# A two-layer model on one core: the second layer's mixer in three groups instead of two, in units tied to the expert stream

## The chip, the cores and the metric

The kernel runs on one core of a Trainium2 chip: TensorE (PE, with its weight loads as PEld), VectorE (DVE), ScalarE (ACT), GpSimd (POOL), SyncE (SP), and 16 DMA engines that all transfers share. The metric is the device time of one execution in microseconds.

## The reference

1024 tokens of width 1024 pass two layers and a last norm. Each layer is a mixer, then a feed-forward over experts ("PEER"). The first mixer is a gated linear recurrence (HGRN2), the second a stick-breaking attention over keys and values that are computed once from the first layer's output. Cut to what matters:

```python
for l in range(2):
    hn = modulate(rms_norm(h, norm_mix_g[l]), sh1, sc1)
    mix = hgrn2_mixer(hn, ...) if l == 0 else stick_breaking_mixer(hn, k_sh, v_sh, sb_w_q, sb_w_out)
    h = h + g1 * mix
    hn = modulate(rms_norm(h, norm_ffn_g[l]), sh2, sc2)
    h = h + g2 * peer_ffn(hn, peer_w_q[l], peer_subkeys[l], peer_u[l], peer_v[l])
    if l == 0:
        k_sh, v_sh = shared_kv(h, ...)       # 8 heads of 128
return rms_norm(h, final_norm_g)

def peer_ffn(xn, w_q, subkeys, u, v):        # per token: 4 heads x 16 experts of 16384
    sc = einsum(xn @ w_q, subkeys)           # 128 scores for each of 2 halves
    s1, i1 = top_k(sc[0], 16); s2, i2 = top_k(sc[1], 16)
    best, flat = top_k(s1[:, None] + s2[None, :], 16)
    w = softmax(best) * gelu(xn . u[expert])
    return sum(w * v[expert])

def stick_breaking_mixer(xn, k, v, w_q, w_out):   # block i of 128 queries sees key blocks 0..i
    z = q @ k.T;  a = exp(z + reversed cumulative sums of log_sigmoid(-z))
    return (a @ v) @ w_out
```

## The kernel before

The tokens are eight blocks of 128. Two things run side by side.

*The expert stream* (`peer_start`, `peer_rep`, `peer_quarter`) goes through the blocks of layer 0, then of layer 1, 16 blocks in all, each in four quarters of 32 tokens. A quarter gathers 16 times 128 table rows of 8 KB (u and v side by side), so 64 quarters make 1024 gathers of 1 MB. GpSimd issues a gather (L690) into a row tile `g`, VectorE multiplies the u half with the token's row `hq` and sums (L692), ScalarE makes Gelu and the scaled selection matrix `sel` for a pair of gathers (L694, L696), and TensorE adds the v half into `va` with four matmuls per gather, called sums here (L699). The tile is then free for a later gather. There are seven row tiles. Once a quarter ScalarE copies the rows of the next quarter's 32 tokens (L668).

*The rest* makes what the stream needs: the first mixer in groups of blocks (`G0`, `hgrn_group`, with routing in `mix_route`), and for the second layer `attn_group`. That one normalizes a group's blocks, projects queries (L730), then for each of eight heads projects keys (L747) and values (L751) of the group's blocks, stores them in DRAM for the later group (`kD`, `vD`), reads the older ones back, and runs `attn_head` for each block (L768 to L784). `mix_out` projects the output and adds it to `h`; `route_group` computes the routing scores (L552, L557) and `best_of` searches the 16 best on VectorE. Keys and values of a head, with two work areas, fill one head tile `K` of 16 KB per partition; there are two. Weights go through four `wt` tiles, 512 KB a load.

The order of instructions on each engine is made when the program is built: a list scheduler takes, among what it thinks ready, the instruction with the smallest priority, and `at(t)` sets the priority of what is written next. The stream's quarters carry the times of `pos`, 100 us ahead of a schedule of 207 us per block; a group's parts carry times spread evenly over its window in `W1`. `tc.issue_after(ins)` puts each instruction of the block behind `ins`, if it runs on the same engine as `ins`; it adds no wait.

Of the kernel before, what the change touches and what calls it, by code (L numbers as in the profile page):

```python
# [15 lines left out]
ALU = mybir.AluOpType  # L16
# [4 lines left out]
G0 = [[0, 1], [2, 3, 4], [5, 6, 7]]  # L21
G1 = [[0, 1, 2, 3], [4, 5, 6, 7]]
GH, GMAX = 3, 4
TAIL = 2
# [7 lines left out]
W0 = [(5, 230), (250, T0 + 2 * PERIOD - 25), (T0 + 1.8 * PERIOD, T0 + 5 * PERIOD - 60)]  # L32
W1 = [(T0 + 4.7 * PERIOD, T0 + 8.2 * PERIOD), (T0 + 7.9 * PERIOD, T0 + 11.8 * PERIOD)]


@with_exitstack
def tile_model(ctx, tc, x, cin, small, ada, w_in, w_out, kvada, kvw, sbq, sbo, wq, subk, tab0, tab1, out):
# [8 lines left out]

    BUFS = dict(wt=4, h=8, T=2, K=2, g=7, hn2=1, hq=2, gs=1, st=1)
    PBUFS = dict(ps=2, pj=2, po=1, pq=1, va=2)
# [38 lines left out]
    last = {}  # L87
# [198 lines left out]

    def mix_out(oT, blocks, w_ap, l, t0, t1):
        n = len(blocks)
        at(t0)
        for half in range(2):  # L290
            at(t0 + (t1 - t0) * half / 2)
            gsb = mix_row(l, half)
            ws = [wload(w_ap[4 * half + c]) for c in range(4)]
            for i, b in enumerate(blocks):
                at(t0 + (t1 - t0) * (half * n + i) / (2 * n))
                ps = bank()
                for c in range(4):
                    for k in range(8):
                        T.matmul(ps[:, blk(c)], lhsT=oT[:, k, blk(i)], rhs=ws[c][:, k, :], start=(k == 0), stop=(k == 7))  # L299
                V.tensor_tensor(out=ps, in0=gsb, in1=ps, op=ALU.mult)  # L300
                hh = hts[b][:, 512 * half:512 * half + 512]
                V.tensor_tensor(out=hh, in0=hh, in1=ps, op=ALU.add)

# [34 lines left out]
    def mix_route(oT, blocks, gsb, spare, t0, t1):  # L338
# [6 lines left out]
        held = spare + spare2 + parts(ktile())  # L345
        early_ws = []
        if blocks == G0[0]:
            work = [hts[7 - i] for i in range(n)]
            early_ws = hts[2:6]
        else:  # L350
            p = parts(ktile())
            work = p[:n]
            held += hts[blocks[-1] + 1:] + p[n:]
            early_ws = held[8:]
# [11 lines left out]

        early = 1 if len(held) >= 8 else n
        for half in range(2):
# [41 lines left out]
    def best_of(l, b, sc):  # L410
        eg = sm("eg", [128, 2, 64], bufs=GMAX)
        for j in range(8):
            if j % 2 == 0:
                s, ix = sm("s", [128, 2, 16]), sm("ix", [128, 2, 16], U32)
            top16(s[:, j % 2, :], ix[:, j % 2, :], sc[:, j], sc[:, j])
            if j % 2:
                pick(eg, j // 2, s, ix)
        R[l, b] = route(l, b, eg)
# [118 lines left out]

    def route_group(l, blocks, t0, t1):
        at(t0)
        n = len(blocks)  # L540
# [6 lines left out]
        for j in range(8):  # L547
            at(t0 + 0.4 * (t1 - t0) * j / 8)
            w = wload(wq[l, j])
            ps = bank("pj")  # L550
            for k in range(8):
                T.matmul(ps[:, 0:128 * n], lhsT=w[:, k, :], rhs=hT[:, k, 0:128 * n], start=(k == 0), stop=(k == 7))  # L552
            qr = sm("qr", [128, 128 * GMAX], bufs=1)
            S.copy(qr[:, 0:128 * n], ps[:, 0:128 * n])
            ps = bank()
            for i in range(n):
                T.matmul(ps[:, blk(i)], lhsT=qr[:, blk(i)], rhs=skt[:, j, :], start=True, stop=True)  # L557
            for i in range(n):
                S.copy(sc[i][:, j], ps[:, blk(i)])
        for i, b in enumerate(blocks):  # L560
            at(t0 + (t1 - t0) * (0.1 + 0.9 * i / n))
            best_of(l, b, sc[i])
# [110 lines left out]
    def peer_quarter(l, b, q):  # L673
# [6 lines left out]
        for c in range(0, 16, NC):  # L680
# [16 lines left out]
            for k in range(NC):  # L697
                for m in range(4):
                    T.matmul(va[32 * m:32 * m + 32, 0:256], lhsT=sel[:, k, :], rhs=ts[k][:, 1024 + 256 * m:1280 + 256 * m], start=(c + k == 0), stop=(c + k == 15))  # L699
        V.tensor_tensor(out=va[:, 0:256], in0=gates[l], in1=va[:, 0:256], op=ALU.mult)  # L700
# [11 lines left out]

    def attn_group(blocks, t0, t1):
        at(t0)
        d = t1 - t0
        n = len(blocks)
# [8 lines left out]
        for j in range(8):  # L725
            at(t0 + d * (0.02 + 0.09 * j / 8))
            w = wload(sbq[j])
# [5 lines left out]
        for i in range(n):  # L733
            norm_T(hs[i], hT[:, :, blk(n - 1 - i)], modk[:, 8:16], modk[:, 0:8], rev=True)
        for hd in range(8):
            at(t0 + d * (0.12 + 0.58 * hd / 8))
            kt = ktile()
# [17 lines left out]
            for i, b in enumerate(blocks):  # L755
                attn_head(b, qT[:, hd, blk(i)], kh, vh, th, st)
        mix_out(qT, blocks, sbo, 1, t0 + 0.7 * d, t0 + 0.8 * d)
        route_group(1, blocks, t0 + 0.8 * d, t1)

# [57 lines left out]

    order = [(l, b) for l in range(2) for b in range(8)]
    with tc.issue_after(norm00[0]):
        peer_start(*order[0])  # L820
    peer_rep(*order[0], 0)
    for n, (l, b) in enumerate(order):
        for q in range(4):
# [5 lines left out]
            peer_quarter(l, b, q)  # L829
        for grp, w in zip(G1, W1):  # L830
            if l == 0 and grp[-1] == b:
                attn_group(grp, *w)

# [63 lines left out]
```

## Time and profile before

| | |
|---|---|
| median of three runs | 3625.27 us (3622.58 to 3629.86) |
| profiled execution, its time | 3632.76 us |
| its span | 3631.1 us |
| PE busy | 2585.4 us, 71% |
| DVE busy | 2600.6 us, 72% |
| ACT, POOL busy | 1127.5 us, 1523.5 us |
| moved by DMA | 1272.86 MB, of it 1073.81 MB by gathers |
| mean granted TensorE clock | 0.805 |

No engine is busy for more than three quarters of the span, but the share of each changes from one stretch to the next, so a share over the whole span names no limit.

### The profile page before, as it was taken

To read this page: it belongs to the slowest core of one execution; us is meant where nothing else is said; L and a number is where in the kernel's file an instruction comes from. 1 tells how busy PE (TensorE), PEld (TensorE's weight loads), DVE (VectorE), ACT (ScalarE), POOL (GpSimd) and SP (SyncE) were. 2 spreads that over 40 slices of the span, in tenths; PEclk is the share of its full clock that TensorE was granted. 3 is DMA by queue.
4 is the path that set the end of the run, shared out by engine and by line. 5 is a ranking of instruction groups with operands and counts; after the bars stand their busy time and mean duration, and the time that the engine had idled before them with its cause. 6 is when DMAs were issued, how large, how long until landed. Compare 5 with 4: busy or idle time off the path is not lost.

```text
span 3631.1 us, 52700 instructions
## 1 busy us (share of the span) xinstructions
PE 2585.4 (71%) x18916; PEld 1654.3 (46%) x18916; DVE 2600.6 (72%) x6229; ACT 1127.5 (31%) x2959; POOL 1523.5 (42%) x1691
## 2 busy tenths in 40 slices
PE   5787999878998888988933488788797333343433
PEld 4686666665767745557411135455573111111111
DVE  7949777599776896665799546766757985565555
ACT  2114332233322443333333233333333232222221
POOL 3322656335664333224334433343343444444443
PEclk8898999899999999999955589899998555555555
DMA  9845989897999899888889988887898899999998
GB/s 394 347 143 221 354 344 359 336 352 303 358 361 365 337 344 372 326 337 328 342 349 353 414 352 351 346 328 309 320 381 345 333 373 409 419 415 418 416 416 349
DMA packets 203878, 1272.86 MB, mean 351 GB/s; under 512 B 22626, under 2 KB 22754, under 8 KB 72547
## 3 DMA queue, kind: packets, MB, share of 16 engines
q0 software_dynamic: 147456, 1073.81, 74.6%
q1 hardware_dynamic: 56162, 195.69, 14.3%
q8 instruction: 152, 2.49, 0.3%
q14 instruction: 108, 0.88, 0.1%
HBM read 1261.02 MB, written 8.39 MB: 350 GB/s over the span
## 4 chain that ended last, share of the span: by engine, by line
PE 42%; DVE 28%; issue 13%; POOL 6%; DMA 6%; ACT 5%; POOLq 0%; SPq 0%; DVEq 0%; ACTq 0%; another core or an unknown queue 0%
DVE g L692 8%; PE pj L445 7%; PE va L699 6%; POOL g L690 5%; DMA g<-in_tab_dram,ev 5%; PE pj L730 3%; PE ps L299 3%; PE pj L747 3%; PE pj L552 3%; PE ps L362 2%; ACT hq L668 2%; PE pj L751 2%; PE pj L449 2%; PE po L783 2%; DVE g L215 2%
## 5 line engine op out<-in xcount | busy, mean ns | idle before, releaser
L690 POOL DMA_INDIRECT g<-in_tab_dram,ev x1024 | 1200.7, 1173 | 1720.1 <-PE va L699 1129.0
L692 DVE SCALAR_TENSOR_TENSOR g<-g,hq 128x1024 f32<-128x1024 f32 x1024 | 1260.7, 1239 | 298.7 <-DMA g<-in_tab_dram,ev 287.5
L699 PE MATMUL va<-g,sel 128*32 128x256 f32 x8192 | 751.0, 499 | 772.4 <-ACT sel L696 764.3
L699 PEld LDWEIGHTS va<-g,sel 128*32 128x32 f32 x8192 | 256.7, 132 | 1191.5 <-ACT sel L696 989.3
L694 ACT ACTIVATE w<-hid 128x2 f32<-128x2 f32 x512 | 104.2, 204 | 1293.2 <-DVE g L692 1274.5
L445 PE MATMUL pj<-T,wt 128*128 128x384 f32 (+1 forms) x1152 | 358.7, 462 | 0.0
L668 ACT COPY hq<-hn 32x1024 f32<-32x1024 f32 x256 | 266.8, 1042 | 44.6 <-DVE g L692 40.4
L696 ACT ACTIVATE sel<-dg,w 128x32 f32<-128x32 f32 x1024 | 273.0, 314 | 15.6
L445 PEld LDWEIGHTS pj<-T,wt 128*128 128x128 f32 x1152 | 216.6, 195 | 101.3 <-issue 7.2
L685 DVE TENSOR_TENSOR dg<-delta,gt 128x128 f32<-128x128 f32 x256 | 78.1, 305 | 179.7 <-ACT sel L696 179.2
L494 POOL TENSOR_TENSOR K<-K,F 128x384 f32<-128x384 f32 (+1 forms) x144 | 151.4, 1071 | 52.9 <-DVE T L466 35.4
L215 DVE SCALAR_TENSOR_TENSOR g<-g,hn 128x1024 f32<-128x1024 f32 x104 | 129.2, 1266 | 6.1 <-DMA g<-in_ada_dram 6.1
L449 PE MATMUL pj<-wt,T 128*128 128x128 f32 x1024 | 127.5, 280 | 0.7 <-ACT K L451 0.6
L751 PE MATMUL pj<-wt,T 128*128 128x128 f32 x1024 | 126.3, 277 | 0.0
L751 PEld LDWEIGHTS pj<-wt,T 128*128 128x128 f32 x1024 | 120.0, 192 | 12.7 <-issue 10.6
L449 PEld LDWEIGHTS pj<-wt,T 128*128 128x128 f32 x1024 | 120.5, 194 | 8.8 <-issue 3.7
L299 PE MATMUL ps<-wt,T 128*128 128x128 f32 x1024 | 123.8, 280 | 0.0
L299 PEld LDWEIGHTS ps<-wt,T 128*128 128x128 f32 x1024 | 118.3, 194 | 11.3 <-issue 9.5
L747 PE MATMUL pj<-T,wt 128*128 128x512 f32 x256 | 120.3, 619 | 0.0
L730 PE MATMUL pj<-T,wt 128*128 128x512 f32 x256 | 117.3, 610 | 2.1 <-DVE T L277 2.1
L552 PE MATMUL pj<-T,wt 128*128 128x512 f32 x256 | 116.2, 604 | 0.5 <-DVE T L277 0.5
L783 PE MATMUL po<-K 128*128 128x128 f32 x576 | 104.5, 329 | 15.4 <-ACT K L781 14.9
(239 smaller groups left out, 3896.2 us busy)
## 6 DMA issues: line engine op xcount, KB each, us to landing
wt<-in_w_in_dram SPq DMA_DIRECT2D x96, 512.0 KB
g<-in_ada_dram SPq DMA_DIRECT2D x88, 512.0 KB
g<-in_tab_dram,ev POOLq DMA_INDIRECT x1024
wt<-in_kvw_dram SPq DMA_DIRECT2D x32, 512.0 KB
wt<-in_w_out_dram SPq DMA_DIRECT2D x18, 512.0 KB
wt<-in_wq_dram SPq DMA_DIRECT2D x17, 512.0 KB
g<-in_kvada_dram SPq DMA_DIRECT2D x16, 512.0 KB
wt<-in_sbq_dram SPq DMA_DIRECT2D x16, 512.0 KB
```

The costliest lines, as they stand in the source:

```text
L299: T.matmul(ps[:, blk(c)], lhsT=oT[:, k, blk(i)], rhs=ws[c][:, k, :], start=(k == 0), stop=(k == 7))
L445: T.matmul(pw, lhsT=w[:, k, :], rhs=hT[:, k, 0:W], start=(k == 0), stop=(k == 7))
L449: T.matmul(ps[:, blk(i)], lhsT=hT[:, k, blk(i)], rhs=w[:, k, :], start=(k == 0), stop=(k == 7))
L552: T.matmul(ps[:, 0:128 * n], lhsT=w[:, k, :], rhs=hT[:, k, 0:128 * n], start=(k == 0), stop=(k == 7))
L668: S.copy(t[32 * j:32 * j + 32, :], hn2[32 * q:32 * q + 32, :])
L690: G.indirect_dma_start(out=t, out_offset=None, in_=tab, in_offset=bass.IndirectOffsetOnAxis(ap=ev[:, q, c + k:c + k + 1], axis=0))
L692: V.scalar_tensor_tensor(u, u, 1.0, hq, op0=ALU.mult, op1=ALU.mult, accum_out=hid[:, k:k + 1])
L696: S.activation(sel[:, k, :], dg[:, c % 4 + k, :], AF.Copy, scale=wt[:, k:k + 1])
L699: T.matmul(va[32 * m:32 * m + 32, 0:256], lhsT=sel[:, k, :], rhs=ts[k][:, 1024 + 256 * m:1280 + 256 * m], start=(c + k == 0), stop=(c + k ...
L730: T.matmul(ps[:, 0:W], lhsT=w[:, k, :], rhs=hT[:, k, 0:W], start=(k == 0), stop=(k == 7))
L747: T.matmul(ps[:, 0:W], lhsT=w[:, k, :], rhs=hT[:, k, 0:W], start=(k == 0), stop=(k == 7))
L751: T.matmul(ps[:, blk(i)], lhsT=hT[:, k, blk(i)], rhs=w[:, k, :], start=(k == 0), stop=(k == 7))
```

## The change

- `G1` is three groups, blocks 0 to 2, 3 to 5, and 6 and 7, where there were two of four blocks. `GMAX` falls from 4 to 3, and with it the size of the tiles `T`, which hold a group's transposed rows.
- `K` has three tiles instead of two, the row tiles `g` are six instead of seven.
- `attn_group` is a generator of twelve units: norms and queries, eight heads, two halves of the output projection, routing. From quarter 17, 29 and 41 on (counted from 0), each group gives one unit per quarter, written behind the quarter's instructions with the priority of the quarter's end, and with its TensorE instructions behind the last sum of that quarter (`last["va"]`).
- In the first layer `mix_route` takes one more head tile for early loads of weights (not for the last group); the part `early` gets is 1, 1 and n as before.

The diff, cut to its core:

```diff
-G1 = [[0, 1, 2, 3], [4, 5, 6, 7]]
-GH, GMAX = 3, 4
+G1 = [[0, 1, 2], [3, 4, 5], [6, 7]]
+GH, GMAX = 3, 3
-W1 = [(T0 + 4.7 * PERIOD, T0 + 8.2 * PERIOD), (T0 + 7.9 * PERIOD, T0 + 11.8 * PERIOD)]
+S1 = [17, 29, 41]
-    BUFS = dict(wt=4, h=8, T=2, K=2, g=7, hn2=1, hq=2, gs=1, st=1)
+    BUFS = dict(wt=4, h=8, T=2, K=3, g=6, hn2=1, hq=2, gs=1, st=1)
...
+        if blocks != G0[2]:
+            held += parts(ktile())
...
-        early = 1 if len(held) >= 8 else n
+        early = 1 if len(held) > 8 else n
...
-                    T.matmul(va[32 * m:32 * m + 32, 0:256], lhsT=sel[:, k, :], rhs=ts[k][:, 1024 + 256 * m:1280 + 256 * m], start=(c + k == 0), stop=(c + k == 15))
+                    last["va"] = T.matmul(va[32 * m:32 * m + 32, 0:256], lhsT=sel[:, k, :], rhs=ts[k][:, 1024 + 256 * m:1280 + 256 * m], start=(c + k == 0), stop=(c + k == 15)).ins
...
+        yield
         for hd in range(8):
-            at(t0 + d * (0.12 + 0.58 * hd / 8))
...
                 attn_head(b, qT[:, hd, blk(i)], kh, vh, th, st)
-        mix_out(qT, blocks, sbo, 1, t0 + 0.7 * d, t0 + 0.8 * d)
-        route_group(1, blocks, t0 + 0.8 * d, t1)
+            yield
+        for half in range(2):
+            mix_half(qT, blocks, sbo, 1, half)
+            yield
+        route_group(1, blocks)
+        yield
...
+    work = [(first, attn_group(grp)) for first, grp in zip(S1, G1)]
...
-        for grp, w in zip(G1, W1):
-            if l == 0 and grp[-1] == b:
-                attn_group(grp, *w)
+            slot = 4 * n + q
+            for first, group in work:
+                if slot >= first:
+                    at(T0 + PERIOD * (slot + 1) / 4)
+                    with after("va"):
+                        next(group, None)
```

What this does to TensorE's order is seen at two places. The first is a head of the second group before: its key projection (`pj`, 512 columns) and value projection stand among the sums of the stream (`va`), whichever quarter these belong to.

```order
L780 MATMUL ps_16536<-ident,K_16411 128x128 x3
L783 MATMUL po_16529<-K_16411 128x128 x4
L747 MATMUL pj_16586<-T_15996,wt_16583 128x512 x8
L783 MATMUL po_16529<-K_16411 128x128 x2
L699 MATMUL va_19384<-g_19452,sel_19451 32x256 x4
L699 MATMUL va_19384<-g_19455,sel_19451 32x256 x4
L699 MATMUL va_19384<-g_19474,sel_19473 32x256 x4
L699 MATMUL va_19384<-g_19477,sel_19473 32x256 x4
L783 MATMUL po_16529<-K_16411 128x128
L751 MATMUL pj_16599<-wt_16596,T_15996 128x128 x14
```

In the change a head's unit of the first group (lines have moved: sums are L694, keys L740, values L744) begins right behind the last sum of one quarter (`va_11529`) and ahead of the first pair of the next (`va_11799`); three pairs of sums farther on its values are done, and the last pairs of the quarter have nothing ahead of them.

```order
L694 MATMUL va_11529<-g_11684,sel_11680 32x256 x4
L740 MATMUL pj_11706<-T_10878,wt_11704 128x384 x8
L744 MATMUL pj_11719<-wt_11717,T_10878 128x128 x2
L694 MATMUL va_11799<-g_11805,sel_11804 32x256 x4
L694 MATMUL va_11799<-g_11808,sel_11804 32x256 x4
L744 MATMUL pj_11719<-wt_11717,T_10878 128x128 x2
L694 MATMUL va_11799<-g_11825,sel_11824 32x256 x4
L694 MATMUL va_11799<-g_11828,sel_11824 32x256 x4
L744 MATMUL pj_11719<-wt_11717,T_10878 128x128 x20
L765 MATMUL pj_11746<-K_11703,T_10781 128x128
```

The second place is TensorE's order in quarter 47, the last of block 3 of layer 1. Before, the second layer's other work is behind it there, and only sums and a row for the stream's own input are left.

```order
L699 MATMUL va_21718<-g_21724,sel_21723 32x256 x4
L699 MATMUL va_21718<-g_21727,sel_21723 32x256 x4
L184 MATMUL pq_22256<-ident,modc_167 128x128 x4
L699 MATMUL va_21718<-g_21744,sel_21743 32x256 x4
L699 MATMUL va_21718<-g_21747,sel_21743 32x256 x4
L699 MATMUL va_21718<-g_21766,sel_21765 32x256 x4
```

In the change a head of the third group stands there, between the pairs of sums.

```order
L740 MATMUL pj_20848<-T_19454,wt_20845 128x256 x8
L744 MATMUL pj_20861<-wt_20858,T_19454 128x128
L694 MATMUL va_20999<-g_21005,sel_21004 32x256 x4
L694 MATMUL va_20999<-g_21008,sel_21004 32x256 x4
L744 MATMUL pj_20861<-wt_20858,T_19454 128x128 x5
L694 MATMUL va_20999<-g_21025,sel_21024 32x256 x4
L694 MATMUL va_20999<-g_21028,sel_21024 32x256 x4
L744 MATMUL pj_20861<-wt_20858,T_19454 128x128 x10
L765 MATMUL pj_20879<-K_20844,T_19357 128x512
L765 MATMUL pj_20882<-K_20844,T_19357 128x384
```

On SP's queue the second group of the change both reads stored keys and values and writes its own, so reads into a head tile, writes out of one and weight loads take turns. Before, the group that read wrote nothing.

```order
L736 DMA K_16533<-kD 128x384
L736 DMA K_16533<-vD 128x384
L94 DMA wt_16548<-in_kvw_dram 128x1024
L747 DMA vD<-K_15933 128x384
L736 DMA K_16908<-kD 128x384
L736 DMA K_16908<-vD 128x384
L94 DMA wt_16909<-in_kvw_dram 128x1024
L747 DMA kD<-K_16233 128x384
L94 DMA wt_16923<-in_kvw_dram 128x1024
```

A write stands ahead of loads for the heads that follow.

## Rows read from the trace of the kernel before

**Rows 1.** Stretches: PE, PEld, DVE, ACT, POOL busy us (records); clock; DMA share; GB/s.

```profile
300.00:1322.00 1022.00, 904.09 (x6817) 654.78 (x6817) 822.12 (x2148) 354.30 (x926) 506.67 (x653) 0.94 0.87 335
1322.00:1776.00 454.00, 404.55 (x2846) 262.14 (x2844) 291.55 (x686) 158.37 (x417) 155.37 (x144) 0.95 0.90 344
1776.00:1982.00 206.00, 96.64 (x699) 41.05 (x698) 198.43 (x695) 66.45 (x167) 80.95 (x69) 0.62 0.90 348
1982.00:2104.00 122.00, 48.86 (x432) 17.01 (x432) 70.23 (x129) 32.17 (x88) 57.98 (x52) 0.53 1.00 404
2104.00:2770.00 666.00, 571.39 (x3966) 366.60 (x3966) 433.73 (x798) 234.71 (x617) 252.69 (x212) 0.93 0.86 338
2770.00:2966.00 196.00, 76.01 (x624) 28.88 (x622) 185.97 (x647) 57.07 (x145) 83.38 (x70) 0.57 0.90 348
2966.00:3600.00 634.00, 251.74 (x2148) 83.12 (x2144) 367.43 (x662) 163.29 (x456) 292.88 (x269) 0.52 1.01 415
```

**Rows 2.** The same stretches, gather issues alone (L690): the count stands in brackets.

```profile
1322.00:1776.00 454.00, 143.93 (x128) 0.95 0.90 344
1776.00:1982.00 206.00, 78.33 (x65) 0.62 0.90 348
1982.00:2104.00 122.00, 57.02 (x50) 0.53 1.00 404
2104.00:2770.00 666.00, 239.25 (x190) 0.93 0.86 338
2770.00:2966.00 196.00, 80.86 (x65) 0.57 0.90 348
2966.00:3600.00 634.00, 285.57 (x251) 0.52 1.01 415
```

**Rows 3.** Timeline around a key projection: start, us, what, [idle before and releaser].

```profile
2354.69 7.98 PE L747 MATMUL pj<-T,wt 128*128 128x512 f32 x16
...
2363.99 0.94 POOL L690 DMA_INDIRECT g<-in_tab_dram,ev  x1 [13.26 <-PE va L699]
...
2370.83 1.22 DVE L692 SCALAR_TENSOR_TENSOR g<-g,hq 128x1024 f32<-128x1024 f32 x1
```

**Rows 4.** Waits: GpSimd's in 2104 to 2770, VectorE's for landings in 300 to 1322.

```profile
POOL g L690 <- PE va L699: 290.8, 64, 13.9
...
DVE g L692 <- DMA g<-in_tab_dram,ev: 7.8, 7, 2.8
```

**Rows 5.** Stretches, sums alone (L699): PE, PEld busy, clock, DMA share.

```profile
1322.00:1776.00 454.00, 73.03 (x1010) 27.42 (x1010) 0.95 0.90 344
2104.00:2770.00 666.00, 107.66 (x1520) 41.36 (x1520) 0.93 0.86 338
2966.00:3600.00 634.00, 239.00 (x2004) 73.88 (x2000) 0.52 1.01 415
```

**Rows 6.** DMA issues by SP: KB each.

```profile
wt<-in_kvw_dram SPq DMA_DIRECT2D x32, 512.0 KB
...
kD<-K SPq DMA_DIRECT2D x8, 256.0 KB
```

**Rows 7.** Groups by line, TensorE, 2104 to 2770 (four blocks): busy, mean ns, idle before.

```profile
L730 PE MATMUL pj<-T,wt 128*128 128x512 f32 x128 | 58.2, 606 | 0.0
...
L270 PE MATMUL ps<-ident,K 128*128 128x128 f32 x40 | 8.2, 362 | 6.9 <-ACT T L275 4.7 <-ACT K L256 1.7 <-DVE h L302 0.4
```

**Rows 8.** Timeline of the stream alone, with the row copies of a quarter.

```profile
3204.16 1.26 POOL L690 DMA_INDIRECT g<-in_tab_dram,ev  x1 [2.44 <-PE va L699]
...
3205.88 1.23 DVE L692 SCALAR_TENSOR_TENSOR g<-g,hq 128x1024 f32<-128x1024 f32 x1 [1.26 <-DMA g<-in_tab_dram,ev]
...
3209.14 1.27 POOL L690 DMA_INDIRECT g<-in_tab_dram,ev  x1 [2.47 <-PE va L699]
...
3212.37 4.20 ACT L668 COPY hq<-hn 32x1024 f32<-32x1024 f32 x4
...
3218.97 0.96 POOL L690 DMA_INDIRECT g<-in_tab_dram,ev  x1 [0.33 <-PE va L699]
```

More of the change, by code (lines that the diff above doesn't have):

```diff
@@ L285, in mix_row, with mix_half @@
         return g
[L287 to L302, printed above, removed]
+    def mix_half(oT, blocks, w_ap, l, half):
+        gsb = mix_row(l, half)
+        ws = [wload(w_ap[4 * half + c]) for c in range(4)]
+        for i, b in enumerate(blocks):
+            ps = bank()
+            for c in range(4):
+                for k in range(8):
+                    T.matmul(ps[:, blk(c)], lhsT=oT[:, k, blk(i)], rhs=ws[c][:, k, :], start=(k == 0), stop=(k == 7))
+            V.tensor_tensor(out=ps, in0=gsb, in1=ps, op=ALU.mult)
+            hh = hts[b][:, 512 * half:512 * half + 512]
+            V.tensor_tensor(out=hh, in0=hh, in1=ps, op=ALU.add)
     state = unit("st", (128, 8, 128))
@@ L410, in best_of @@
     def best_of(l, b, sc):
-        eg = sm("eg", [128, 2, 64], bufs=GMAX)
+        eg = sm("eg", [128, 2, 64], bufs=4)
         for j in range(8):
@@ L536, in tile_model, with route_group @@
     norm00, norm7, best0 = [], [], []
-    def route_group(l, blocks, t0, t1):
-        at(t0)
+    def route_group(l, blocks):
         n = len(blocks)
@@ L547, in route_group @@
         for j in range(8):
-            at(t0 + 0.4 * (t1 - t0) * j / 8)
             w = wload(wq[l, j])
@@ L560, in route_group @@
         for i, b in enumerate(blocks):
-            at(t0 + (t1 - t0) * (0.1 + 0.9 * i / n))
             best_of(l, b, sc[i])
@@ L711, in tile_model, with attn_group @@
     vD = dp.tile([8, 128, 8, 128], F32, name="vD")
-    def attn_group(blocks, t0, t1):
-        at(t0)
-        d = t1 - t0
+    def attn_group(blocks):
         n = len(blocks)
@@ L725, in attn_group @@
         for j in range(8):
-            at(t0 + d * (0.02 + 0.09 * j / 8))
             w = wload(sbq[j])
```

## Prediction

> **What bounds the kernel now.** Start with the table of stretches [rows 1] and read one column at a time. In the last stretch and in the short one at 1982 the DMA share is 1.00 to 1.01: nothing else matters there. The gathers issued in these two [rows 2], 50 and 251 in 122 and 634 us, give the price of one gather at full DMA rate, 756/301 = 2.51 us, so 40.2 us for a quarter of 16. Elsewhere the DMA share is 0.86 to 0.90, and each stretch has another limit. In 1322 to 1776 and 2104 to 2770 it is TensorE: busy 404.55 of 454 and 571.39 of 666 us, at a granted clock of 0.95 and 0.93, with VectorE at 64 and 65%. In 1776 to 1982 and 2770 to 2966 it is VectorE, 198.43 of 206 and 185.97 of 196 us: the top-16 searches of four blocks. The first layer, 300 to 1322, has TensorE at 88% and VectorE at 80%.
>
> What each stretch costs beyond 2.51 us per gather, from the counts in [rows 2]: the two TensorE stretches 454 - 128 x 2.51 = 132.7 and 666 - 190 x 2.51 = 189.1, together 321.8 us; the two VectorE stretches 206 - 65 x 2.51 and 196 - 65 x 2.51, together 75.7 us.
>
> How a TensorE stretch loses its time is seen in one place [rows 3]. At 2354.69 a head's key projection occupies TensorE for 7.98 us; the sums queued behind it come after it, and only at 2363.99 can GpSimd, idle for 13.26 us, reuse a row tile and issue a gather. The total of that wait in the second stretch is 290.8 us [rows 4].
>
> **The change, part by part.**
>
> *Spreading.* TensorE's second-layer work is what is not a sum in the two stretches: 404.55 - 73.03 and 571.39 - 107.66 [rows 1, 5], 795 us. It is not made smaller: three groups do the same blocks with the same columns. It now lies in 36 quarters (three times twelve units), 22 us each. A quarter's sums are 128 records (a matmul stands as two in this profile) of 107.66/1520 us at the high clock, 9.1 us. So 31 us of TensorE against 40.2 of gathers: TensorE is no longer the limit of a light quarter, and the 321.8 us fall away, if nothing else takes their place. What does is priced next.
>
> *Loads.* Three groups instead of two load every second-layer weight a third time: 16 for the key and value weights, 8 each for query, output and routing queries, 1 for subkeys, so 41 of 512 KB [rows 6] or 21.5 MB. The stored keys and values go from 32 transfers of 256 KB to 32 writes and 16 reads of 192 KB and 16 reads of 384 KB, 15.7 for 8.4 MB. The second layer's loads are then 123 x 0.524 + 15.7 = 80.2 MB. Behind a busy TensorE their time was covered; in quarters that DMA limits it is not: 80.2 MB at 415 GB/s [rows 1] is 193 us. The VectorE stretches left a tenth of 402 us of DMA free; half of that, 20 us, I let cover loads: +173. Ends: 69 us (only the 28.8 MB that are new count) and 193. On SP a write of stored keys waits for ScalarE's copy, and weight loads of the next heads stand behind it, as the order shows; four weight tiles and three head tiles keep these a head ahead, so I add nothing. A load that came late all the same would hold one key projection and the sums behind it.
>
> *First units.* Query projection and transposes of three blocks are one unit. From [rows 7] the projection is 58.2 x 3/4 = 43.7 us and 24 transposes and 24 reversals, priced alike at 8.2/40, are 9.8; with the sums 63 us, 16 above a light quarter of some 47. For the first group I count it whole, for the others half, as these quarters are VectorE's (the searches of the group before) anyway: +32. Ends 0 and 48.
>
> *Searches.* The same VectorE work in three bursts: 75.7 us as now.
>
> *Six row tiles.* In [rows 8] the cycle of a pair is seen at full DMA rate: a pair's first gather is issued at 3204.16, the next pair's at 3209.14, 5.0 us later. How short could a tile's cycle be? With an almost empty queue a gather issued at 2363.99 is multiplied at 2370.83 [rows 3], 6.84 us; its partner lands 2.51 later; and from the second multiply (3205.88) to the next issue (3209.14) [rows 8] are 3.26 us. Sum 12.6. Six tiles are three pairs, 15.06 us at full rate, so 2.5 us are to spare; seven tiles had 17.57, so 5.0. Once a quarter the four copies that spread the next quarter's rows stand on ScalarE ahead of the pair's weights: 4.20 us at 3212.37, and the next issue comes at 3218.97 instead of some 3214.1. Seven tiles cover 4.2 us, six leave 1.7 open. There are 46 quarters from 18 on (counted from 0); without 8 that VectorE limits: +66. Ends 0 (the spare is larger than I measured) and, if ScalarE's and VectorE's other waits also come through, the rival below.
>
> The Trainium skill has a fixed price for such a transfer: "DMA: Bandwidth & Descriptors", section on the anatomy of one DMA by the GpSimd path, gives about 2.0 us plus bytes over 436e3, estimated 4.4 us for a 1 MB gather. By it the cycle would be some 10.2 us, six tiles would cover the copies, and the forecast would be 66 us lower. The trace has 6.84 us up to the multiply, and its number is the one used.
>
> *Key projections behind the quarter's last sum.* In the change they stand where the order shows them, once a quarter, 7.98 x 3/4 = 6.0 us (4.0 in the group of two). The first pair of sums is due 5.0 us after the last one, so about 1 us is late: 24 x 1 = +24. Ends 0 and, if each still cost the 13.26 - 5.0 us of [rows 3], 198.
>
> *First layer.* Six row tiles and a third head tile. VectorE waited for a gather's landing only 7.8 us in those 1022 [rows 4]: gathers lie ready, so one tile less should cost nothing. TensorE's order holds the same work ahead of quarter 16; it is idle 118 us, of which a third head tile might return a third. I take 0, ends -40 and +50; the startup loads, which find two half row tiles fewer, and the routing weights, which find four more places, lie inside these ends.
>
> *Sum.* -322 + 173 + 32 + 66 + 24 = -27 us. The profiled execution took 3632.8 us, so 3606; it stands 7.5 us above the median of the three runs, which gives **3598 us**.
>
> **Rivals.**
>
> *All cheap (faster).* Six tiles and the projections cost nothing, and half of the first units: 3598 - 66 - 24 - 16 = 3492; half-way to that is 3545. For it: VectorE's few waits in the first layer. Against: at full rate it waits for each landing already [rows 8].
>
> *Nothing gained.* Loads, first units and tiles eat up what spreading frees: 27 us more of costs than I count, which is one more microsecond in each light quarter. 3625.
>
> *Six tiles make the second layer wait (slower).* In 2104 to 2770 one gather takes 666/190 = 3.5 us, so a tile's cycle was 7 x 3.5 = 24.5 us, twice the 12.6 it could be; the rest is waiting in the queues of TensorE, ScalarE and VectorE [rows 4]. A light quarter of 47.4 us needs a cycle of at most 6 x 47.4/16 = 17.8 us. That is where it decides: each microsecond above adds 16/6 = 2.7 us to a quarter, 80 us over some 30 light quarters. At 18.9, still nearer to 12.6 than to 24.5, the kernel takes 3598 + 85 = 3683.
>
> *The clock (slower).* In the stretches without second-layer work TensorE's granted clock is 0.52 to 0.62, the lower of its levels (1.2 of 2.4 GHz) nearly throughout, and a sum costs 239.00/2004 us instead of 107.66/1520 [rows 5], 1.68 times as much. If light quarters ran so, TensorE would need 31 x 1.68 = 52 us in each, 4.7 more than 47.4, and over 30 of them 140. Against it: a projection is a dense run, and in [rows 1] such work ran at 0.93 and 0.95. With half of it at the low level: 3598 + 70 = 3668.
>
> The Trainium skill, "TensorE: Matmul & The Clock Gate", section on HAM oscillation in real kernels, speaks against the change here: matmul chunks shorter than the DMA waits between them run at the throttled clock, chunk after chunk. By it the whole 140 us would come; the trace shows the low clock only where sums stand alone.
>
> **How the numbers follow.** The forecast and its neighbourhood, 3570 to 3617, gets 0.38; cheap, below 3570, 0.16; nothing gained, within 0.2% of 3625 (about what a measurement of this kernel can tell from no change), 0.11; six tiles 0.22; clock 0.13. So faster 0.54, same 0.11, slower 0.35. The range 3510 to 3700 leaves one in ten at each end: below lies most of "all cheap" together, above the full price of the clock or a cycle over 19 us. If it is faster, 3530 to 3617.
>
> **What the new profile would show.** Right: DMA share 0.95 or more in most of the second layer outside the searches, GpSimd's wait for sums without pieces of 13 us, quarters of some 47 us in the light ones, and the end of the run at full DMA rate with little above 41 us a quarter. Wrong: VectorE waiting for landings with a DMA share below 0.9 (six tiles); sums at over 0.11 us each and a clock near 0.5 in the light quarters (clock); a first layer that ends later than now, at which I look first; or searches that are not done when the second layer's stream reaches their blocks, which would stop the gathers outright.

## The result and the profile after

The changed kernel takes 3678.84 us (median of four runs, 3672.47 to 3684.18) beside 3627.57 us for the kernel before in the same comparison: a ratio of 1.0148, interval [1.0135, 1.0161]. It is slower, where 3598 was forecast. The time is near that of the rival in which six row tiles make the second layer wait, 3683, but it did not come about in that way, as the section on the prediction shows. The profiled execution took 3676.5 us, its span is 3674.7.

In the view of stretches the second layer of the changed kernel, from 1323 on, falls into light quarters (one unit of a group in each) and short bursts, in which searches and the first unit of the next group lie. The columns are those of [rows 1]: PE, PEld, DVE, ACT, POOL busy; clock; DMA share; GB/s.

```profile
300.00:1323.00 1023.00, 883.73 (x6694) 639.83 (x6694) 827.93 (x2194) 338.73 (x893) 505.89 (x647) 0.92 0.87 335
1323.00:1471.00 148.00, 106.83 (x716) 59.28 (x717) 85.23 (x174) 48.73 (x129) 58.04 (x50) 0.80 0.93 367
1471.00:1966.00 495.00, 332.27 (x2508) 205.75 (x2508) 286.10 (x593) 149.65 (x407) 193.48 (x177) 0.75 0.96 374
1966.00:2150.00 184.00, 151.59 (x937) 91.97 (x935) 164.96 (x551) 71.89 (x177) 53.98 (x50) 0.90 0.88 339
2150.00:2601.00 451.00, 328.53 (x2504) 216.42 (x2505) 287.50 (x541) 151.46 (x404) 184.54 (x164) 0.83 0.96 374
2601.00:2785.00 184.00, 132.35 (x895) 90.29 (x893) 166.22 (x541) 65.17 (x168) 64.85 (x53) 0.86 0.89 345
2785.00:3125.00 340.00, 215.94 (x1726) 145.98 (x1726) 214.73 (x362) 104.78 (x278) 141.41 (x119) 0.78 0.96 380
3125.00:3279.00 154.00, 93.86 (x740) 61.48 (x740) 118.69 (x362) 50.44 (x133) 61.44 (x57) 0.75 0.95 372
3279.00:3640.00 361.00, 135.34 (x1136) 43.78 (x1136) 210.53 (x413) 87.78 (x247) 163.06 (x144) 0.51 0.97 391
```

The same stretches behind the first layer with the gather issues alone (L685 here), the count in brackets, answer to [rows 2]:

```profile
1323.00:1471.00 148.00, 57.07 (x48) 0.80 0.93 367
1471.00:1966.00 495.00, 185.00 (x161) 0.75 0.96 374
1966.00:2150.00 184.00, 52.15 (x48) 0.90 0.88 339
2150.00:2601.00 451.00, 175.06 (x144) 0.83 0.96 374
2601.00:2785.00 184.00, 61.40 (x48) 0.86 0.89 345
2785.00:3125.00 340.00, 138.05 (x112) 0.78 0.96 380
3125.00:3279.00 154.00, 57.98 (x48) 0.75 0.95 372
3279.00:3640.00 361.00, 159.89 (x136) 0.51 0.97 391
```

Read the DMA share first. Before, the stretches with second-layer work showed 0.86 and 0.90 and TensorE was busy for 86 to 89% of them; now the light ones show 0.96 and TensorE is busy for 64 to 73%. The work has been spread as intended and no other engine is at its limit, yet the DMA engines are not full either. In the last stretch, where the stream runs alone, the share was 1.01 and is now 0.97: 361 us for 136 gathers is 42.5 us a quarter, where [rows 1, 2] give 634/251 x 16 = 40.4.

By the ledger of the prediction (time less 2.51 us per gather):

- the three light stretches, 1286 us and 417 gathers: 239 us, 49.3 us a quarter. At the 47.4 that I forecast they would have cost 188;
- the two bursts at 1966 and 2601: 127; the start at 1323 and the third burst at 3125: 27.5 and 33.5. Together 188, where the forecast left 168 (371 less the 188 above and 15 for the last stretch);
- the last stretch: 19.6, forecast 15.

So 51 + 20 + 5 = 76 us too much, of which some 5 came back elsewhere: the profiled time is 70 us above the 3606 that the sum gave for it. The first layer ends as before: the first 260 gathers are issued by 1268 us, before it was 261 by 1269.

What is missing in a light quarter is read from the waits in 1471 to 1966 (engine, line, waited for: us, times, longest).

```profile
POOL g L685 <- PE va L694: 204.6, 56, 8.9
...
DVE g L687 <- DMA g<-in_tab_dram,ev: 116.7, 83, 7.2
```

VectorE waits 116.7 us for landings while the DMA engines have a share of 0.96: gathers are issued too late, since GpSimd waits for row tiles. One quarter's start in the timeline shows how.

```profile
1763.25 0.95 POOL L685 DMA_INDIRECT g<-in_tab_dram,ev  x1 [0.30 <-issue]
...
1764.89 4.20 ACT L663 COPY hq<-hn 32x1024 f32<-32x1024 f32 x4
...
1769.12 0.53 ACT L691 ACTIVATE sel<-dg,w 128x32 f32<-128x32 f32 x2
...
1769.49 1.94 PE L694 MATMUL va<-g,sel 128*32 128x256 f32 x16 [7.34 <-ACT sel L691]
...
1771.36 6.76 PE L740 MATMUL pj<-T,wt 128*128 128x384 f32 x16
...
1771.39 0.53 ACT L691 ACTIVATE sel<-dg,w 128x32 f32<-128x32 f32 x2
...
1771.49 0.97 POOL L685 DMA_INDIRECT g<-in_tab_dram,ev  x1 [0.33 <-PE va L694]
...
1773.24 1.00 POOL L685 DMA_INDIRECT g<-in_tab_dram,ev  x1 [0.17 <-issue]
...
1778.49 1.07 PE L694 MATMUL va<-g,sel 128*32 128x256 f32 x16
...
1779.43 0.95 POOL L685 DMA_INDIRECT g<-in_tab_dram,ev  x1 [5.20 <-PE va L694]
```

ScalarE copies the next quarter's rows for 4.20 us; only then come the weights (1769.12), and TensorE has sat idle for 7.34 us when the last sums of the quarter start. Behind them the key projection takes 6.76 us (predicted 6.0). The weights of the next pair are ready at 1771.92, yet its sums start only at 1778.49, 6.6 us later. The issue at 1763.25 is the second of a pair, and the next pair's second comes at 1773.24, 10.0 us later; from this pair's first, at 1771.49, to the first of the following one are 7.9 us. 5.0 would keep the DMA engines busy [rows 8]. Here six tiles had no reserve for two such delays on end.

### The profile page after: what moved, and what is told of

Read it like the earlier page. It is cut to its first block, busy times and chain, and to the rows that moved or that the text cites. A ratio compares the mean times of both kernels' runs of the same rounds, so it can differ in the third digit from the quotient of the medians.

```text
span 3674.7 us, 53571 instructions
## 1 busy us (share of the span) xinstructions
PE 2620.5 (71%) x19308; PEld 1761.3 (48%) x19308; DVE 2603.9 (71%) x6229; ACT 1138.4 (31%) x2993; POOL 1533.6 (42%) x1691
## 3 DMA queue, kind: packets, MB, share of 16 engines
q1 hardware_dynamic: 66674, 224.53, 16.2%
q8 instruction: 155, 2.54, 0.3%
## 5 line engine op out<-in xcount | busy, mean ns | idle before, releaser
L685 POOL DMA_INDIRECT g<-in_tab_dram,ev x1024 | 1207.6, 1179 | 1723.9 <-PE va L694 1105.4
L694 PE MATMUL va<-g,sel 128*32 128x256 f32 x8192 | 725.8, 484 | 759.9 <-ACT sel L691 759.3
L694 PEld LDWEIGHTS va<-g,sel 128*32 128x32 f32 x8192 | 250.2, 128 | 1119.8 <-ACT sel L691 952.1
L443 PE MATMUL pj<-T,wt 128*128 128x384 f32 (+1 forms) x1152 | 357.2, 462 | 0.7 <-DVE T L278 0.7
L740 PE MATMUL pj<-T,wt 128*128 128x384 f32 (+1 forms) x384 | 143.7, 527 | 3.7 <-DVE T L278 2.7
L744 PEld LDWEIGHTS pj<-wt,T 128*128 128x128 f32 x1024 | 125.1, 192 | 22.5 <-issue 15.2
L744 PE MATMUL pj<-wt,T 128*128 128x128 f32 x1024 | 132.9, 279 | 0.0
L780 PE MATMUL po<-K 128*128 128x128 f32 x576 | 117.9, 371 | 20.9 <-ACT K L778 20.5
L780 PEld LDWEIGHTS po<-K 128*128 128x128 f32 x576 | 102.6, 269 | 43.0 <-ACT K L778 38.0
L548 PE MATMUL pj<-T,wt 128*128 128x384 f32 (+1 forms) x384 | 118.1, 457 | 6.1 <-DMA wt<-in_wq_dram 3.5
```

Of the source, the lines that this page charges most:

```text
L443: T.matmul(pw, lhsT=w[:, k, :], rhs=hT[:, k, 0:W], start=(k == 0), stop=(k == 7))
L685: G.indirect_dma_start(out=t, out_offset=None, in_=tab, in_offset=bass.IndirectOffsetOnAxis(ap=ev[:, q, c + k:c + k + 1], axis=0))
L694: last["va"] = T.matmul(va[32 * m:32 * m + 32, 0:256], lhsT=sel[:, k, :], rhs=ts[k][:, 1024 + 256 * m:1280 + 256 * m], start=(c + k == 0), ...
L740: T.matmul(ps[:, 0:W], lhsT=w[:, k, :], rhs=hT[:, k, 0:W], start=(k == 0), stop=(k == 7))
L744: T.matmul(ps[:, blk(i)], lhsT=hT[:, k, blk(i)], rhs=w[:, k, :], start=(k == 0), stop=(k == 7))
L780: T.matmul(po[:, 0:128], lhsT=vh[:, 7 - b + j, :], rhs=st[:, blk(j)], start=(j == 0), stop=(j == n - 1))
```

## The experiments

Ratios are to the kernel before on the same chip, in brackets the 95% interval. Runs on different chips are compared by their ratios, a ratio of 0.01 being 36 us. The kernel before itself took 3627.6 to 3644.5 us in these comparisons, so times read from the traces of two of them can differ by 0.5% without meaning anything. "The units" means groups, units and their place behind the sums, as in the change.

**Row tiles and head tiles.** Three kernels keep the units, go back to two head tiles and take six, seven and eight row tiles. Without the third head tile the early loads of the first layer's routing have no extra places, and `early` is n throughout. The first is shown; the others have `g=7` and `g=8`. Eight row tiles and two head tiles fill the same memory as the change's six and three.

```diff
-    BUFS = dict(wt=4, h=8, T=2, K=3, g=6, hn2=1, hq=2, gs=1, st=1)
+    BUFS = dict(wt=4, h=8, T=2, K=2, g=6, hn2=1, hq=2, gs=1, st=1)
...
-        if blocks != G0[2]:
-            held += parts(ktile())
...
-        early = 1 if len(held) > 8 else n
+        early = n
```

Six row tiles:

> The change with two head tiles instead of three and still six row tiles (the first layer's early weight loads go back to their old places, and all of a group's output halves are done before its routing). It is the control for the next two. Theory (six row tiles cost the second layer its gain): 3665 to 3700, like the change, since the row tiles are the same. Rival (the third head tile was what the change needed): above 3700, with the second layer's heads waiting for a tile.

Measured 3706.52 us, 1.0221 [1.0204, 1.0238], just above 3700 and so in the range of the rival. What was missing is shown further down: not the tile for the heads, but the places for early loads.

Seven:

> The same with seven row tiles, as many as before. Theory (six row tiles): 65 to 75 us less than with six: the ten quarters at the end go from 43 back to 41 us (20 us), some 29 light quarters from 49 to 47.5 (45 us); about 3610. Rival (row tiles do not matter; the loads of a third group and the quarters in which searches and first units meet do): within 15 us of the control.

Measured 3599.09 us, 0.9923 [0.9907, 0.994], a gain of 107 us where 65 to 75 were expected.

Eight:

> The same with eight row tiles, in the memory that the kernel before used. Theory (six row tiles): a little below the one with seven, 3590 to 3610, because four whole pairs are in flight; the DMA share of light quarters near 1.00. Rival: within 15 us of the control.

Measured 3576.40 us, 0.9856 [0.984, 0.9873], below the expected range.

One tile is worth 107 us from six to seven, 23 from seven to eight. The stretch of ten light quarters (20 to 29) is shown by the view of stretches, for each kernel the row of all engines, then that of its gather issues. Six tiles:

```profile
1485.00:1982.00 497.00, 333.71 (x2487) 208.14 (x2487) 281.70 (x581) 149.56 (x407) 190.28 (x175) 0.74 0.94 368
1485.00:1982.00 497.00, 180.96 (x159) 0.74 0.94 368
```

Seven:

```profile
1458.00:1926.00 468.00, 326.52 (x2503) 204.26 (x2504) 283.70 (x591) 149.35 (x407) 190.09 (x176) 0.77 0.99 395
1458.00:1926.00 468.00, 178.90 (x160) 0.77 0.99 395
```

Eight:

```profile
1473.00:1924.00 451.00, 324.68 (x2509) 205.35 (x2510) 281.95 (x591) 149.78 (x408) 192.77 (x176) 0.79 1.00 406
1473.00:1924.00 451.00, 181.62 (x160) 0.79 1.00 406
```

The busy times of the engines hardly differ; the DMA share goes from 0.94 to 0.99 and 1.00, a quarter from 50.0 to 46.8 and 45.1 us. These counts are good to one gather, 0.3 us a quarter; from the first gather of quarter 20 to that of quarter 30 the traces give 50.4, 46.4 and 45.5. VectorE's waits for landings in the three stretches fall with it; the row of each, in the same order, from three answers:

```profile
DVE g L685 <- DMA g<-in_tab_dram,ev: 111.1, 78, 6.2
```

```profile
DVE g L685 <- DMA g<-in_tab_dram,ev: 60.6, 47, 4.0
```

```profile
DVE g L685 <- DMA g<-in_tab_dram,ev: 37.3, 30, 2.2
```

Not all of the 107 us lie there. The gathers issued by the end of the first layer, with six tiles and with seven:

```profile
0.00:1292.00 1292.00, 296.53 (x260) 0.92 0.83 322
0.00:1257.00 1257.00, 306.54 (x261) 0.93 0.85 329
```

So 35 us are lost in the first layer, 72 behind it.

The two later light stretches behave otherwise. With seven tiles, quarters 33 to 40 and 44 to 51, all engines and then gather issues:

```profile
2085.00:2485.00 400.00, 298.94 (x2372) 205.56 (x2370) 259.03 (x463) 132.06 (x354) 164.89 (x142) 0.86 0.96 377
2654.00:3046.00 392.00, 261.22 (x2012) 175.21 (x2010) 267.37 (x489) 128.75 (x334) 173.60 (x138) 0.80 0.95 375
2085.00:2485.00 400.00, 157.39 (x128) 0.86 0.96 377
2654.00:3046.00 392.00, 168.48 (x128) 0.80 0.95 375
```

That is 50.0 and 49.0 us a quarter, 3 us more than in the ten quarters above, though no tile is missing. Eight tiles have 49.4 and 48.9 there, six 51.7 and 50.1, the changed kernel 50.6 and 49.6.

**Six row tiles in the kernel before**, nothing else changed.

```diff
-    BUFS = dict(wt=4, h=8, T=2, K=2, g=7, hn2=1, hq=2, gs=1, st=1)
+    BUFS = dict(wt=4, h=8, T=2, K=2, g=6, hn2=1, hq=2, gs=1, st=1)
```

> The kernel before with six row tiles instead of seven and nothing else. Theory (six row tiles): the some 22 quarters at full DMA rate take 2 to 2.5 us more each, 50 us, and the quarters that TensorE limits a little more: 3675 to 3720. Rival (row tiles do not matter): 3620 to 3640.

Measured 3697.64 us, 1.0195 [1.0178, 1.0212]. So 70 us without any units: the seventh tile was worth that much already, and 107 with the units in. Here too the first 260 gathers come late, by 1285 us (before: 261 by 1269).

**The row copies on VectorE**, in the changed kernel (six tiles), in the kernel before (seven) and with eight tiles.

```diff
-            S.copy(t[32 * j:32 * j + 32, :], hn2[32 * q:32 * q + 32, :])
+            V.tensor_copy(t[32 * j:32 * j + 32, :], hn2[32 * q:32 * q + 32, :])
```

> The change with six row tiles, the four row copies of a quarter moved from ScalarE to VectorE; nothing else. Theory (the copies ahead of the pair's weights are what six tiles no longer cover): 2 us less in each of some 38 quarters, 3600 to 3620, and the last quarters at 41 us instead of 43. Rival (all waits of the pair's chain count, the copies are a small part of them): 3660 to 3690.

Measured 3653.86 us, 1.0021 [1.0009, 1.0034], 46 us below the change's 1.0148, and between the ranges of theory and rival. The ten light quarters:

```profile
1490.00:1959.00 469.00, 339.53 (x2517) 209.60 (x2516) 314.97 (x643) 108.76 (x371) 197.38 (x176) 0.76 1.00 397
1490.00:1959.00 469.00, 189.79 (x160) 0.76 1.00 397
```

46.9 us a quarter, as with seven tiles, where the changed kernel has 495/161 x 16 = 49.2. In these ten quarters the edit is worth about as much as a seventh tile. In the two later light stretches it gains next to nothing: 50.4 and 49.7 us a quarter, where the changed kernel has 50.6 and 49.6. In the first layer the edit cost time: 259 gathers by 1288 us, where the changed kernel has 260 by 1268.

> The kernel before, with seven row tiles, the row copies on VectorE instead of ScalarE. Theory: seven tiles cover them at full DMA rate, so no gain there, and VectorE, which limits two stretches, gets 0.7 us times four a quarter more: 0.998 to 1.010. Rival (copies cost in themselves): 0.985 to 0.990.

Measured 3647.17 us, 1.0013 [1.0004, 1.0023]: with seven tiles it gains nothing in all. But 259 gathers are out only by 1288 us (before: 261 by 1269), so what is lost in the first layer is gained behind it.

> The version with eight row tiles, the row copies on VectorE instead of ScalarE. Theory (the copies cost only where too few tiles are in flight; with six they cost 46 us of the change's 3679): eight tiles cover them, so within 15 us of the 0.9856 times the kernel before that the version without the move has, 0.982 to 0.990. Rival (copies on ScalarE cost in themselves, whatever the tiles): 0.972 to 0.978.

Measured 3578.95 us, 0.9825 [0.9808, 0.9841], 0.3% below eight tiles with the copies on ScalarE; the two intervals overlap, from two chips. Here too the first layer ends later, and a quarter of the first light stretch takes 44.5 us instead of 45.5. So seven or eight tiles do not make the copies free; that they cost only where tiles are few is not shown.

**The copies on the engine that is freer in each layer**: with eight tiles, ScalarE for the stream's layer 0, VectorE for its layer 1.

```diff
-            S.copy(t[32 * j:32 * j + 32, :], hn2[32 * q:32 * q + 32, :])
+            (V.tensor_copy if l else S.copy)(t[32 * j:32 * j + 32, :], hn2[32 * q:32 * q + 32, :])
```

> Three groups in units, eight row tiles, two head tiles; the row copies stand on ScalarE in the first layer and on VectorE in the second. Theory: with all copies on VectorE quarter 16 began at about 1277 us instead of 1263, because VectorE is busier than ScalarE in the first layer, and the stretch behind it gave more than that back; so with each layer's copies on its freer engine quarter 16 begins near 1263 again, the later gain stays, and the ratio is some 0.4% below the 0.9825 of all copies on VectorE: 0.978 to 0.980. Rival: the later start is not due to the copies, or what is won before quarter 16 is lost behind it since the loads only move: ratio 0.982 to 0.985.

Measured 3565.35 us, 0.9795 [0.978, 0.9811], the fastest of all: 0.3% below all copies on VectorE, as expected, with intervals that just touch. 260 gathers are issued by 1270 us, where with all copies on VectorE it was 254. So the copies on VectorE gain behind the first layer and lose within it, and each layer wants its own engine.

**Which part of the third head tile gave time back.** The changed kernel against the same with two head tiles is 1.0148 against 1.0221. Here the third tile stays and only the extra places for early loads go.

```diff
-        if blocks != G0[2]:
-            held += parts(ktile())
...
-        early = 1 if len(held) > 8 else n
+        early = n
```

> The changed kernel with its three head tiles and six row tiles, without the one more head tile that the first layer's routing takes for early loads. With two head tiles and no such places the ratio was 1.0221, with both 1.0148. If the third head tile itself gives the 28 us: 1.013 to 1.016. If the places for early loads give them: 1.020 to 1.024. Between 1.016 and 1.020 both have a part.

Measured 3713.54 us, 1.0219 [1.0195, 1.0242]: the same as with two head tiles. The tile as such gives nothing; the places, with the smaller `early` that they allow, give all of the 0.7%, some 26 us. At 1268 us 254 gathers are out instead of 260.

**Second-layer loads doubled**, with eight tiles: each weight load of the second layer is issued twice into the same tile, 64.5 MB more (nothing else changes).

```diff
+    def wload2(ap):
+        t = unit("wt")
+        load(t, ap)
+        load(t, ap)
+        return t.rearrange("p (k n) -> p k n", k=8)
...
-                w = wload(kvw[j])
+                w = wload2(kvw[j])
```

> The version with eight row tiles, with each second-layer weight load issued twice into the same tile: 123 loads more, 64.5 MB. Theory (in these quarters loads cost their full time on the DMA engines, 155 us at 415 GB/s, less what the search quarters hide): 130 to 170 us more than without, 3705 to 3745. Rival (a third or more of the loads' time is still hidden): less than 100 us more, under 3675.

Measured 3700.52 us, 1.0165 [1.0148, 1.0183], 3.1% or 112 us above eight tiles, between the 130 to 170 of the theory and the 100 of the rival. The queue of the loads shows the bytes, 289.02 MB where the changed kernel has 224.53:

```profile
q1 hardware_dynamic: 84386, 289.02, 20.3%
```

64.5 MB at 415 GB/s are 155 us, so 72% of the transfer time is paid.

**The units without their place behind the sums**, with eight tiles.

```diff
-                    with after("va"):
-                        next(group, None)
+                    next(group, None)
```

> The version with eight row tiles, without the rule that puts a unit's TensorE instructions behind the last sum of its quarter; units, quarters and priorities stay. Theory (the spreading over quarters is what gains, the rule adds little): within 20 us of the version with it, 3557 to 3597. Rival (the rule is the gain, since it keeps projections from standing ahead of sums): 40 us or more slower.

Measured 3638.36 us, 0.9993 [0.9983, 1.0002], 50 us slower than with it. I had held that the spread priorities alone would do; they don't. Two stretches, all engines, then the gather issues of the first:

```profile
1387.00:1910.00 523.00, 440.96 (x3160) 301.67 (x3158) 377.95 (x1022) 192.40 (x504) 179.18 (x163) 0.92 0.91 351
2733.00:3143.00 410.00, 164.19 (x1420) 55.10 (x1420) 257.18 (x516) 109.83 (x299) 189.89 (x172) 0.52 1.00 413
1387.00:1910.00 523.00, 168.27 (x145) 0.92 0.91 351
```

The scheduler takes the units early: TensorE is 84% busy in the first stretch (57.7 us a quarter), and in the second only sums are left. That is the shape of the kernel before.

**The groups' starts moved apart**, with eight tiles: the first group starts one quarter earlier, the third one later. This was meant to leave a gap between searches and first units.

```diff
-S1 = [17, 29, 41]
+S1 = [16, 29, 42]
```

> The version with eight row tiles and groups that begin at quarters 16, 29 and 42 instead of 17, 29 and 41, so that a quarter lies free between a group's routing and the next group's first unit. Theory (the nine quarters around searches lose by searches and first units meeting, some 35 us in each of the first two places): 20 to 40 us less, 3535 to 3560. Rival (VectorE's searches alone set these quarters): within 10 us.

Measured 3597.75 us, 0.9879 [0.9863, 0.9895], not faster. Five quarters around the second burst (28 to 32), gather issues, in this kernel:

```profile
1841.00:2121.00 280.00, 89.34 (x79) 0.84 0.91 356
```

and with eight tiles, starts as in the change:

```profile
1827.00:2108.00 281.00, 88.72 (x80) 0.87 0.93 361
```

The total is the same, but the edit did not make the gap. The searches of the first group (one of their instructions, with its first and last start) and the query projection of the second group's first unit, in the kernel with the moved starts:

```profile
L562 DVE FIND_INDEX8 flat<-eg,cand x12: 406/414/422, 1888.8 to 2031.2; 128x8 uint32<-128x256 f32 x12
L721 PE MATMUL pj<-T,wt x128: 486/486/590, 1990.4 to 2041.3; 128*128 128x384 f32 x128
```

For 41 of its 51 us the projection still runs beside searches. Whether the two hide each other is therefore not shown by this run.

## Why the prediction was wrong

The step that failed is the price of a light quarter apart from its row tiles: the 321.8 us of *Spreading* fall away, and only *Loads* (4.8 us a quarter) and *Key projections* (0.7) take their place, the same in each of the three groups. That makes 45.7 us, the 47.4 less the 1.7 for six tiles. The kernel with seven tiles tests it, since it lacks no tile: without the +66 the sum is -93, so 3532 us, and it took 3599. (It has two head tiles and no extra places for early loads; a third head tile without the places changed nothing, 1.0219 against 1.0221.) The place is seen when the first layer is left out. From the first gather of quarter 16 to the end of the span the traces give 2379.4 us before, 2350.3 with seven tiles, 2426.2 with six row tiles and two head tiles, 2415.7 in the change. These are single executions, good to some 10 us.

- *Seven tiles against before*: -29 where the sum without the row tiles has -93. So 64 us are missing that no row tile explains.
- *The change against seven tiles*: +65, and +76 for six tiles with two head tiles, where *Six row tiles* has +66. In total that term was right to 10 us behind the first layer.

So the missing tile is why the change is slower than the kernel before, for with it back the units gain 28 us; but the forecast had paid for it.

The light quarters hold all of the 64: with seven tiles 46.4, 50.0 and 49.0 us in the three stretches against 45.7, which is 7 + 34 + 26 = 67 us over. What stood in the place of the sum's price can be read in part, for the stretch of the second group:

```profile
q0 software_dynamic: 18375, 133.82, 84.4%
q1 hardware_dynamic: 6883, 16.58, 11.4%
```

The 16 gathers of a quarter (q0) keep the DMA engines busy for 84.4% of 50.0 us, 42.2 us, where 40.2 were counted; other transfers, nearly all of them loads and stored keys and values (q1), take 5.7 instead of 4.8; and the engines are idle for 2.0 us, where the key projections had 0.7. In the third stretch the idle time is some 2.5 us. What leaves them idle stays open: an eighth tile, or the copies on VectorE in the changed kernel, move these two stretches by at most 0.7 us a quarter; only the eighth tile and the copies on VectorE together take the third from 49.0 to 46.8, and leave the second at 48.8.

The rival *Six row tiles make the second layer wait* has nearly the measured time, by luck: it put another 85 us on the row tiles, and they cost at most 10 more than forecast. Its condition does not speak for it, since 6 x 1286/417 = 18.5 us is the length of a light quarter in other units, whatever makes it long.

The other terms, point by point:

- *Six row tiles*, where: I priced 1.7 us for each of 38 quarters. Against seven tiles the change has 3.0 us in each of the ten quarters of the first stretch (49.3 beside 46.4), some 0.5 in the two later ones, and 1.8 in quarters 55 to 62. So the total is right in part by chance. In the first stretch the copies are most of it; six tiles do not account for all of what they cost there, since with eight the same edit still takes 1.0 us from a quarter.
- *First layer, 0*: right by luck. I counted nothing, because VectorE waited only 7.8 us for landings [rows 4]. Six tiles cost 35 us there with the units and 16 in the kernel before. The wait shows that gathers lay ready with seven tiles, not how many tiles that took. That the first layer of the change ended where it did before was two effects that cancelled, the tile against the early loads.
- *Spreading, -322*: the gain is there, its size is not shown by itself. With seven row tiles, as before, the units bring the ratio to 0.9923; some of that lies in the first layer, which ends 12 us sooner (261 gathers by 1257 us, before by 1269) and whose `early` differs. It rests on the place behind the sums, 50 us, which I had taken as part of the spreading without pricing it.
- *Loads, +173*: too low in two of three stretches, as above, and too even. The first stretch moves 15.7 MB on q1 in ten quarters, the second 16.6 in eight. For bytes added throughout the second layer 72% is paid; how the price divides between loads and gathers that share the DMA engines is not shown.
- *First units, +32, and searches, 75.7*: counted by whole quarters (17 to 19, 30 to 32, 41 to 43, 52 to 54) the bursts and their surroundings cost 178 us beyond 2.51 per gather where the forecast left 168, and with seven tiles 160, so the difference goes with the row tiles. Whether searches hide half a first unit stays open.
- *Key projections, +24*: the first pair was to be due 5.0 us after the last sums, so only 1 us late. In quarters 20 to 26 of the change its sums start 5.9 to 8.6 us after its weights are ready; the timeline above is one of these. With seven and eight tiles the pair is about as late. What that costs depends on the tiles in reserve, and no run separates it.
- *The clock rival*: the granted clock did fall, to 0.75 to 0.83 in the light stretches, and a sum alone took 117.35/1280 = 0.092 us, between the 0.071 and 0.119 of [rows 5].

```profile
1471.00:1966.00 495.00, 117.35 (x1280) 39.97 (x1280) 0.75 0.96 374
```

But at 0.79 with eight tiles the DMA share is 1.00, so the clock did not set the time in that stretch; in the two dearer stretches it was higher, 0.86 and 0.80 with seven tiles beside 0.77. "TensorE: Matmul & The Clock Gate" in the Trainium skill, section on HAM oscillation, had spoken for the low clock throughout; the trace agrees in direction, not in extent, and its price did not come.

The Trainium skill's price of a gather, "DMA: Bandwidth & Descriptors", section on the anatomy of one DMA, would have left six row tiles without a cost. The trace of the kernel before has 6.84 us to the multiply against the 4.4 estimated from it (VectorE was at other work just before, so the landing can be a little earlier), so it is too short for the way up to the consumer, and the runs have 65 to 76 us for the tile.

What also stays open: why the eighth tile gains more than nothing in the first stretch when seven already show a share of 0.99 (0.9 us of a quarter's 46.4), and how the 50 us of the place behind the sums divide among the engines.

## What to carry to other kernels

When a sum misses, give back one term at a time before blaming the one that looks guilty: here the tile was priced right behind the first layer, and only the kernel with its seventh tile back showed that the price around it was short. A price averaged over groups hides that the later ones are dearer. An engine that seldom waits for landings shows that the buffers suffice, not by how much. An edit that is to pull two things apart has to be seen to do so in the trace. Before memory moves from one pool to another, ask what else could use it: the same memory as eight row tiles and two head tiles made this change 1.4% faster than the kernel before instead of 1.5% slower. Where a stretch comes out unchanged, look for two effects before writing down none.

## What the runs showed of the hardware

- A copy of 32 x 1024 f32 from one set of partitions to another took 0.685 us on VectorE (median of 128), 1.042 on ScalarE. The groups by operation in the fastest kernel (duration in ns: least, median, most):

```profile
L661 ACT COPY hq<-hn x128: 1027/1042/1048, 308.6 to 1940.7; 32x1024 f32<-32x1024 f32 x128
L661 DVE COPY hq<-hn x128: 661/685/755, 1999.0 to 3476.5; 32x1024 f32<-32x1024 f32 x128
```

- A DMA share near 1 leaves room: from 0.99 to 1.00, with a seventh and an eighth tile, the rate in the light quarters went from 395 to 406 GB/s, 2.8%.
- Beside loads a gather took more of the DMA engines: with seven tiles 84.4% of 400 us for 128 gathers, 2.64 us each, in the second light stretch; 98.2% of 331 us for 128, 2.54 each, where the stream ran alone.
- The mean of TensorE's granted clock lay between its two levels over whole stretches (0.74 to 0.83) where runs of 6 to 8 us alternated with sums, and at 0.51 where sums stood alone.
